# Turning attention weights by DMA as two 16-bit planes, and making low halves with an adding DMA

## The chip, the core and the metric

The kernel runs on one core of a Trainium2 chip. The metric is device time in microseconds of one execution. TensorE (PE) does matmuls, VectorE (DVE), ScalarE (ACT) and GpSimd (POOL) do elementwise work, and SyncE (SP) issues most DMAs. PEld is TensorE's weight load.

## The reference

The kernel computes one layer of a hybrid encoder on a sequence of 512 frames with 1024 channels, in float32. The core of the reference, cut to what matters here:

```python
# branch A: sparse attention, per head of 64 channels, in blocks of 128 queries
dots  = einsum('thd,sd->ths', q_idx, k_idx) * IDX_DIM ** -0.5
score = einsum('th,ths->ts', w_idx, relu(dots))            # -inf beyond the query's chunk
_, sel = top_k(score, n_sel)
logits = einsum('thd,tnhd->htn', q, k[sel]) * HEAD_DIM ** -0.5 + bias
p = softmax(logits)
yA = einsum('htn,tnhd->thd', p, v[sel])
# branch B: stick-breaking attention
z = einsum('thd,shd->hts', q, k) * HEAD_DIM ** -0.5
log_keep = where(causal, log_sigmoid(-z), 0)
later = cumsum(log_keep, reverse) - log_keep
a = where(causal, exp(log_sigmoid(z) + later), 0)
yB = einsum('hts,shd->thd', a, v)
# both branches: projection, sigmoid gates, output projection, LayerNorm; then a gated conv FFN, LayerNorm
```

Both branches have eight heads. All their queries, keys, values and gates come from one input projection. A weighing (the last product of each branch) needs the weights with keys on the partitions, so the 512 x 512 triangle of a head's weights, which is computed with queries on the partitions, has to be turned.

## The kernel before

**Products.** Each float32 operand is split into a high half (rounded to the matmul's format) and a low half (the rest). A product is three matmuls: high weight by high x (line 223), high weight by low x (224), low weight by high x (225). Weights come in pieces of 128 x 1024 through the class `Stream`: a load on SP's queue (line 71) into a ring of three `raw` tiles, ScalarE's copy to `whi` (line 101) and a subtraction `wlo = raw - whi` (line 103), in rings of three. The pieces are loaded and split three ahead of their use. For the 19 pieces named in `POOL_LO` (queries, keys and gates of the stick-breaking branch, one query, one key and four value pieces of the sparse one) GpSimd does the subtraction, for all others VectorE.

**Order.** `FILL` lists the projection pieces. Around and between the 16 heads, eight stick-breaking (`s`) ahead of eight sparse ones (`a`), the calls `fill(GAP)` pour 15 of their matmuls. From these the scheduler of the compiler makes each engine's queue by a timeline that it simulates, so small pieces can interleave. A head goes through `start_head` (logits, and for a sparse head the whole softmax), `turn_weights` and `weigh`; head i + 1 is started before head i is turned and weighed.

**Turning and weighing.** A head's weights are 128 x 1280: four query blocks j with 128 (j + 1) key columns each, at the columns `OFF[j]`. `turn_weights` does ten transposes of 128 x 128 on TensorE (line 410) into three PSUM banks (`tr_ps`), and from each bank ScalarE makes a high half `pth` (line 414) and VectorE a low half `ptl` (line 415). `weigh` takes eight matmuls (line 426): for each key block i the columns 128 i to 512 of the queries, high and low. ScalarE and VectorE then add the two column halves into `avt` and `ytmp`.

**The sparse head.** `dsa_head` loads a window of relative biases `win`, GpSimd adds the mask from the selection into `bm` (line 479), TensorE makes the logits `l_ps` (line 490), VectorE adds bias and finds the extreme (494), ScalarE takes the exponential in place (496) and VectorE normalises (502); the result is the tile `lg`.

**A turn by DMA that is already there.** Between attention and FFN the normalised rows `r` are turned as two 16-bit planes: ScalarE copies a plane (line 742, `own`), SP issues a transposing DMA (743, `got`), ScalarE or VectorE copies it back (750, `back`), and the halves `x1h` and `x1l` are made (752, 753).

**Other names.** `ks_ps` and `gb_ps` are PSUM banks of projections; `va` and `vs` are the value tiles, `ga` and `gb` the gates, `ya` and `ys` the weighed pairs of heads. `ln` is LayerNorm's parameters, `s_win` and `s_line` are a DRAM scratch for the relative bias.

Of the kernel before, what the change touches and what calls it, by code (L numbers as in the profile page):

```python
# [11 lines left out]
F32 = mybir.dt.float32  # L12
F32R = mybir.dt.float32r
# [38 lines left out]

class Stream:


    def __init__(self, tc, raw, ring, pieces, ahead_load, ahead_split, place=None, lo_on_pool=()):
# [5 lines left out]
        self.lo_on_pool = set(lo_on_pool)  # L62
# [23 lines left out]
    def _advance(self, upto):  # L86
        nc = self.nc
        n = len(self.pieces)
        self.load(min(n, upto + self.al))
        while self.ns < min(n, upto + self.asp, self.nl):  # L90
            t, w = self.loaded.pop(self.ns)
            key = self.pieces[self.ns][0]
            if key in self.place:
                hi, lo = self.place[key](key)
            else:
                hi = self.ring.tile([128, 1024], F32R, tag="whi", name=f"whi_{self.ns}")
                lo = self.ring.tile([128, 1024], F32R, tag="wlo", name=f"wlo_{self.ns}")
            after = None
            if key in self.prepare:
                w, after = self.prepare[key](t)  # L100
            nc.scalar.activation(hi[:, :w], t[:, :w], AF.Copy)  # L101
            eng = nc.gpsimd if key in self.lo_on_pool else nc.vector
            self.done[key] = eng.tensor_sub(lo[:, :w], t[:, :w], r32(hi[:, :w])).ins  # L103
# [14 lines left out]
def tile_block(ctx: ExitStack, tc: tile.TileContext, xT, xN, w_qi, w_ki, w_t, w_v, w_br, w_o, w_fi, w_fo,  # L118
# [74 lines left out]
    st = Stream(tc, rawp, ring, order, 3, 3, place, POOL_LO)  # L193


    idle = bp.tile([128, 512], mybir.dt.bfloat16, tag="beta", bufs=2, name="idle")
# [5 lines left out]

    ident = cst.tile([128, 128], F32, name="ident")
    make_identity(nc, ident)
    first = bp.tile([128, 512], F32, name="first")
# [157 lines left out]
    def idx_scores():  # L363
        kih, kil, wi = index["k"]
        for j in (1, 2, 3):
            N = 128 * (j + 1)
            for h in range(H):
                yield j
                ps = pa("dot_ps")
                r = slice(j * 128, j * 128 + 128)  # L370
                nc.tensor.matmul(ps[:, :N], qi[h][:, r], kih[:, :N], start=True, stop=False)
                nc.tensor.matmul(ps[:, :N], qi[h][:, r], kil[:, :N], start=False, stop=True)
                rl = bp.tile([128, 512], F32, tag="pt", bufs=8, name="relu")
# [23 lines left out]
            pass  # L397


    def turn_weights(a):  # L400

        groups = (((0, 0),), ((1, 0), (3, 384)), ((2, 0),))
        pth, ptl = {}, {}
        for grp in groups:
            ps = pb("tr_ps")
            width = 0
            for i, o in grp:
# [1 line left out]
                    c = OFF[j] + i * 128  # L409
                    nc.tensor.transpose(ps[:, o + (j - i) * 128:o + (j - i) * 128 + 128], a[:, c:c + 128], ident)  # L410
                width = max(width, o + 512 - 128 * i)
            th = bp.tile([128, 512], F32R, tag="pt", bufs=8, name="pth")
            tl = bp.tile([128, 512], F32R, tag="pt", bufs=8, name="ptl")
            nc.scalar.activation(th[:, :width], ps[:, :width], AF.Copy)  # L414
            lows = nc.vector.tensor_sub(tl[:, :width], ps[:, :width], r32(th[:, :width]))  # L415
            for i, o in grp:
                pth[i] = th[:, o:o + 512 - 128 * i]
                ptl[i] = tl[:, o:o + 512 - 128 * i]
        return pth, ptl, lows.ins

    def weigh(pth, ptl, vt, h, ytmp):

        ps = pb("av_ps")
        seq = [(i, t) for i in range(NB) for t in (pth, ptl)]
        for n, (i, t) in enumerate(seq):
            nc.tensor.matmul(ps[:, 128 * i:512], vt[i][:, h].rearrange("p a d -> p (a d)"), t[i],  # L426
                             start=(n == 0), stop=(n == len(seq) - 1))
# [3 lines left out]
        nc.scalar.activation(tmp[own], ps[oth], AF.Copy)  # L431
        nc.vector.tensor_add(ytmp[own], ps[own], tmp[own])

    def finish_pair(ytmp, name):
        yh = xp.tile([128, 512], F32R, tag="y", bufs=12, name=f"{name}h")
# [36 lines left out]
    def dsa_head(q, k, h):  # L472
# [11 lines left out]
        for grp in ((3,), (0, 2), (1,)):  # L484
            ps = pb("l_ps")
            o = 0
            for j in grp:
                N = 128 * (j + 1)
                for hl in range(2):
                    nc.tensor.matmul(ps[:, o:o + N], q[:, hl, j * 128:j * 128 + 128], k[:, :N],  # L490
                                     start=(hl == 0), stop=(hl == 1))
                c = slice(OFF[j], OFF[j] + N)
                b = win[:, 384:512] if j == 0 else bm[:, c]
                nc.vector.tensor_tensor_reduce(out=lg[:, c], in0=ps[:, o:o + N], in1=b, scale=1.0, scalar=3.0e38,
                                               op0=ALU.add, op1=ALU.min, accum_out=mn[:, j:j + 1])
                nc.scalar.activation(lg[:, c], lg[:, c], AF.Exp, scale=-1.0, bias=mn[:, j:j + 1],
                                     accum_out=sm[:, j:j + 1])
                o += N
        nc.vector.reciprocal(rs, sm)
        for j in range(NB):  # L500
            c = slice(OFF[j], OFF[j] + 128 * (j + 1))
            nc.vector.tensor_scalar(lg[:, c], lg[:, c], rs[:, j:j + 1], None, op0=ALU.mult)
# [83 lines left out]
    def start_head(i):  # L586
# [5 lines left out]
        return sb_head(*args) if w == "s" else (dsa_head(*args),)  # L592

    weights = start_head(0)
    sb_sticks(*weights)
    fill_until("qs1", "ks1")
    for i, (w, h) in enumerate(heads):
        following = start_head(i + 1) if i + 1 < len(heads) else (None,)
        fill(GAP)
        pth, ptl, lows = turn_weights(weights[0])  # L600
        if len(following) == 2:
            with tc.issue_after(lows):
                scan = sb_sticks(*following)
            with tc.issue_after(scan):
                select_some(ROUNDS[i])
        fill(GAP)
        if h % 2 == 0:
            ytmp = bp.tile([128, 512], F32, tag="yt", bufs=2, name=f"y{w}t{h//2}")
        fill_until(f"v{w}")
        weigh(pth, ptl, vals[w], h, ytmp)  # L610
        if h % 2 == 1:
            (ys if w == "s" else ya).append(finish_pair(ytmp, f"y{w}{h//2}"))
# [524 lines left out]
```

## Time and profile before

| | |
|---|---|
| runs, median | 762.77 us (762.73 to 762.9) |
| the profiled execution | 762.16 us |
| its span | 760.4 us |
| granted TensorE clock, mean over the span | 0.998 |
| TensorE busy | 748.6 us, 98% |
| VectorE busy | 555.4 us, 73% |
| ScalarE busy | 379.3 us, 50% |
| GpSimd busy | 153.5 us, 20% |

The stages by time: until 60 us the first loads, index queries and keys; to about 205 us the stick-breaking heads; to about 330 us the sparse heads; then projections of the branches, gates, output projection and the FFN; from 690 us the tail of the FFN and the last LayerNorm. Matmuls overlap: a row's duration is longer than the distance to the next row's start, and what one costs TensorE is read from the starts.

### The profile page before, as it was taken

How to read it: one execution, taken by the hardware profiler on the slowest of the kernel's cores; microseconds unless marked ns; L12 is line 12 of the kernel's file. 1: busy time of each engine (PE TensorE's matmuls, PEld its weight loads, DVE VectorE, ACT ScalarE, POOL GpSimd, SP SyncE). 2: the span in 40 equal slices, each digit the busy share in tenths (PEclk: the TensorE clock that was granted, in tenths of full speed). 3: DMA queues.
4: the chain of work that ended last, by engine and by line, in shares of the span. 5: the costliest groups of instructions: out<-in, count | busy, mean ns of one | idle time of the engine just before them, and what ended most of it. 6: DMA issues, size and time to landing. Idle time of an engine off the chain costs nothing.

```text
span 760.4 us, 9842 instructions
## 1 busy us (share of the span) xinstructions
PE 748.6 (98%) x3573; PEld 627.3 (82%) x3573; DVE 555.4 (73%) x905; ACT 379.3 (50%) x568; POOL 153.5 (20%) x160
## 2 busy tenths in 40 slices
PE   9999999999999999999999999999999999999995
PEld 7878888887888888888889888888888888888885
DVE  5569787799878585548765867766776768668995
ACT  5474756655574756835364633433443344346430
POOL 1002555426644210000111110111011101110012
PEclk9999999999999999999999999999999999999999
DMA  8445433232223324116942344544444444448632
GB/s 267 147 128 181 125 95 96 72 111 84 80 102 111 111 76 122 64 60 206 340 61 84 139 156 136 155 137 139 153 140 142 147 138 137 141 152 274 222 105 79
DMA packets 40448, 102.89 MB, mean 135 GB/s; under 512 B 10888, under 2 KB 11272, under 8 KB 40400
## 3 DMA queue, kind: packets, MB, share of 16 engines
q1 hardware_dynamic: 34672, 85.98, 35.4%
q0 software_dynamic: 3728, 11.04, 4.0%
q10 hardware_dynamic: 2000, 5.24, 2.8%
q8 instruction: 28, 0.46, 0.3%
q14 instruction: 20, 0.16, 0.1%
HBM read 88.59 MB, written 9.98 MB: 130 GB/s over the span
## 4 chain that ended last, share of the span: by engine, by line
PE 92%; DVE 5%; issue 1%; ACT 0%; POOL 0%; POOLq 0%; ACTq 0%; DVEq 0%
PE u_ps L774 5%; PE u_ps L776 5%; PE g_ps L774 5%; PE u_ps L775 5%; PE g_ps L776 5%; PE g_ps L775 5%; PE m L856 2%; PE m L854 2%; PE m L855 2%; PE av_ps L426 2%; PE ga_ps L224 2%; PE ga_ps L223 2%; PE ga_ps L225 2%; PE o_ps L704 2%; PE o_ps L703 2%; PE o_ps L705 2%
## 5 line engine op out<-in xcount | busy, mean ns | idle before, releaser
L101 ACT ACTIVATE whi<-raw 128x1024 fp32r<-128x1024 f32 (+1 forms) x124 | 124.1, 1001 | 169.5 <-PE g_ps L775 44.9
L103 DVE TENSOR_TENSOR wlo<-raw,whi 128x1024 fp32r<-128x1024 f32 (+1 forms) x105 | 120.0, 1144 | 41.3 <-ACT whi L101 40.5
L776 PE MATMUL u_ps<-x1h,wlo 128*128 128x512 f32 (+1 forms) x192 | 71.4, 372 | 0.0
L774 PE MATMUL u_ps<-x1h,whi 128*128 128x512 f32 (+1 forms) x192 | 71.3, 372 | 0.0
L775 PE MATMUL u_ps<-x1l,whi 128*128 128x512 f32 (+1 forms) x192 | 71.3, 371 | 0.0
L774 PE MATMUL g_ps<-x1h,whi 128*128 128x512 f32 (+1 forms) x184 | 69.9, 380 | 0.0
L775 PE MATMUL g_ps<-x1l,whi 128*128 128x512 f32 (+1 forms) x184 | 69.9, 380 | 0.0
L776 PE MATMUL g_ps<-x1h,wlo 128*128 128x512 f32 (+1 forms) x184 | 69.9, 380 | 0.0
L103 POOL TENSOR_TENSOR wlo<-raw,whi 128x1024 fp32r<-128x1024 f32 x19 | 45.8, 2412 | 34.5 <-ACT whi L101 34.4
L776 PEld LDWEIGHTS u_ps<-x1h,wlo 128*128 128x128 f32 x192 | 36.2, 188 | 6.3
L775 PEld LDWEIGHTS u_ps<-x1l,whi 128*128 128x128 f32 x192 | 36.2, 188 | 6.3
L774 PEld LDWEIGHTS u_ps<-x1h,whi 128*128 128x128 f32 x192 | 36.2, 188 | 6.2
L415 DVE TENSOR_TENSOR ptl<-tr_ps,pth 128x512 fp32r<-128x512 f32 (+1 forms) x48 | 27.9, 595 | 18.2 <-ACT pth L414 17.6
L776 PEld LDWEIGHTS g_ps<-x1h,wlo 128*128 128x128 f32 x184 | 34.6, 188 | 6.6
L775 PEld LDWEIGHTS g_ps<-x1l,whi 128*128 128x128 f32 x184 | 34.6, 188 | 6.5
L774 PEld LDWEIGHTS g_ps<-x1h,whi 128*128 128x128 f32 x184 | 34.6, 188 | 6.5
L797 DVE TENSOR_TENSOR t<-raw 128x512 f32<-128x512 f32 x11 | 7.6, 693 | 40.2 <-DMA raw<-in_w_fo_dram 40.2
L816 POOL MEMSET u<- 128x2 f32 x22 | 2.1, 98 | 143.7 <-ACT whi L101 99.9
L830 DVE TENSOR_TENSOR hF<-g_ps,c 128x512 f32<-128x512 f32 x22 | 15.1, 687 | 20.4 <-PE g_ps L776 20.4
L822 ACT ACTIVATE c<-c,cwt 128x512 f32<-128x512 f32 x22 | 16.0, 725 | 26.3 <-DVE c L821 26.1
L672 POOL TENSOR_TENSOR rstd<-rstd,mhalf 128x1 f32<-128x1 f32 x8 | 7.6, 951 | 106.0 <-DVE rstd L671 106.0
L414 ACT ACTIVATE pth<-tr_ps 128x512 fp32r<-128x512 f32 (+1 forms) x48 | 23.9, 520 | 9.8 <-PE tr_ps L410 6.8
(566 smaller groups left out, 2055.9 us busy)
## 6 DMA issues: line engine op xcount, KB each, us to landing
raw<-in_w_fi_dram SPq DMA_DIRECT2D x44, 512.0 KB, 3.3
raw<-in_w_t_dram SPq DMA_DIRECT2D x32, 512.0 KB, 3.4
raw<-in_w_fo_dram SPq DMA_DIRECT2D x26, 512.0 KB, 4.2
raw<-in_w_br_dram SPq DMA_DIRECT2D x8, 512.0 KB, 3.3
raw<-in_w_o_dram SPq DMA_DIRECT2D x8, 512.0 KB, 4.2
raw<-in_w_v_dram SPq DMA_DIRECT2D x7, 512.0 KB, 3.9
raw_b<-in_w_fo_dram SPq DMA_DIRECT2D x6, 512.0 KB, 4.2
s_t<-t POOLq DMA_DIRECT2D x11, 256.0 KB, 2.3
```

What stands on the lines that cost most here:

```text
L101: nc.scalar.activation(hi[:, :w], t[:, :w], AF.Copy)
L103: self.done[key] = eng.tensor_sub(lo[:, :w], t[:, :w], r32(hi[:, :w])).ins
L223: nc.tensor.matmul(ps[:M], wh[:, c], xh[k], start=(k == 0), stop=False)
L224: nc.tensor.matmul(ps[:M], wh[:, c], xl[k], start=False, stop=False)
L225: nc.tensor.matmul(ps[:M], wl[:, c], xh[k], start=False, stop=(k == KC - 1))
L414: nc.scalar.activation(th[:, :width], ps[:, :width], AF.Copy)
L415: lows = nc.vector.tensor_sub(tl[:, :width], ps[:, :width], r32(th[:, :width]))
L426: nc.tensor.matmul(ps[:, 128 * i:512], vt[i][:, h].rearrange("p a d -> p (a d)"), t[i], start=(n == 0), stop=(n == len(seq) - 1))
L774: nc.tensor.matmul(ps[:, c], wh[:, kc], x1h[:, k, c], start=(k == 0), stop=False)
L775: nc.tensor.matmul(ps[:, c], wh[:, kc], x1l[:, k, c], start=False, stop=False)
L776: nc.tensor.matmul(ps[:, c], wl[:, kc], x1h[:, k, c], start=False, stop=(k == KC - 1))
L822: nc.scalar.activation(c, c, AF.Gelu_apprx_tanh, bias=cwt[:, f, 3:4])
```

## The change

**A. The eight sparse heads are turned by DMAs.** The ten transposes and three evictions of a sparse head go. `send_planes`, called at the end of `dsa_head`, copies the high 16 bits of `lg` (ScalarE) and the low 16 bits (VectorE) into the memory of `bm`, and SP issues two transposing DMAs (line 441) into one tile `pl`. `join_planes` copies the planes back into float32 words (`back`), and makes one high and one low half of 128 x 1280 from them. The columns of a sparse head are laid out by `SOFF`, and the transposed blocks of a key block i lie 384 columns apart; the first key block is weighed as 384 and 128 columns, so `weigh` has ten matmuls for a sparse head. A sparse head is now weighed one head later, and its joining is ordered behind the last logits of the following head. The stick-breaking heads are turned on TensorE as before, into one pair of 1280-wide tiles instead of eight 512-wide ones; tiles that used the old ones (`kih`, `kil`, `wiT`, `relu`) take others.

**B. Nineteen low halves come from an adding DMA.** For the pieces now named `DMA_LO` ScalarE writes minus the high half into `wlo` (line 104), and GpSimd issues a DMA (line 105) that reads the weights from DRAM once more and adds them onto it.

```diff
-POOL_LO = [t for t in FILL[4:] if t[:-1] in ("qs", "ks", "gb")] + ["qa0", "ka0"]
-POOL_LO += [f"va{g}" for g in range(4)]
+DMA_LO = [t for t in FILL[4:] if t[:-1] in ("qs", "ks", "gb")] + ["qa0", "ka0"]
+DMA_LO += [f"va{g}" for g in range(4)]
 OFF = {0: 0, 2: 128, 3: 512, 1: 1024}
+SOFF = {1: 0, 0: 256, 2: 384, 3: 768}
...
             nc.scalar.activation(hi[:, :w], t[:, :w], AF.Copy)
-            eng = nc.gpsimd if key in self.lo_on_pool else nc.vector
-            self.done[key] = eng.tensor_sub(lo[:, :w], t[:, :w], r32(hi[:, :w])).ins
+            if key in self.lo_by_dma:
+                nc.scalar.activation(lo[:, :w], r32(hi[:, :w]), AF.Copy, scale=-1.0)
+                self.done[key] = nc.gpsimd.dma_start(lo[:, :w], self.pieces[self.ns][1], accum_op=ALU.add).ins
+            else:
+                self.done[key] = nc.vector.tensor_sub(lo[:, :w], t[:, :w], r32(hi[:, :w])).ins
...
+    def send_planes(lg, bm):
+        src = halves16(lg)
+        own = bm[:, 0:ATT].bitcast(U16).rearrange("p (a c) -> p a c", a=2)
+        pl = bp.tile([128, 2, ATT // 128, 128], U16, tag="pl", bufs=1, name="pl")
+        nc.scalar.activation(own[:, 1], src[:, 1], AF.Copy)
+        nc.vector.tensor_copy(own[:, 0], src[:, 0])
+        for a in (0, 1):
+            nc.sync.dma_start_transpose(pl[:, a], own[:, a])
+        return pl
+
+    def join_planes(pl):
+        back = bp.tile([128, ATT], F32, tag="back", bufs=1, name="back")
+        got = pl.rearrange("p a b c -> p a (b c)")
+        nc.scalar.activation(halves16(back)[:, 1], got[:, 1], AF.Copy)
+        nc.vector.tensor_copy(halves16(back)[:, 0], got[:, 0])
+        th, tl = turned()
+        nc.scalar.activation(th, back, AF.Copy)
+        nc.vector.tensor_sub(tl, back, r32(th))
+        h, l = (t.rearrange("p (s c) -> p s c", c=128) for t in (th, tl))
+        parts = [(i, o, h[:, c], l[:, c]) for i, o, c in
+                 ((0, slice(128, 512), slice(0, 9, 3)), (0, slice(0, 128), slice(2, 3)),
+                  (1, slice(128, 512), slice(1, 9, 3)), (2, slice(256, 512), slice(5, 9, 3)),
+                  (3, slice(384, 512), slice(9, 10)))]
+        return parts
...
+        else:
+            ends = following[2:]
+            if joined is not None:
+                added = values_of(*joined)
+                ends = ends or added
+            fill(GAP)
+            with tc.issue_after(ends[0]), tc.issue_after(ends[1]):
+                parts = join_planes(weights[0])
+            joined = parts, w, h
```

On TensorE, among the last two sparse heads before, a head's transposes stand inside the other's weighing and among gate matmuls (`ga_ps`):

```order
L426 MATMUL av_ps<-ptl,va_2210 128x384
L426 MATMUL av_ps<-pth,va_2213 128x256
L410 MATMUL tr_ps<-ident,lg 128x128 x6
L426 MATMUL av_ps<-ptl,va_2213 128x256
L426 MATMUL av_ps<-pth,va_2216 128x128
L426 MATMUL av_ps<-ptl,va_2216 128x128
L410 MATMUL tr_ps<-ident,lg 128x128 x4
L223 MATMUL ga_ps<-xh_324,whi_3011 128x512
```

In the changed kernel the weighing of such a head on TensorE reads:

```order
L466 MATMUL av_ps<-ptl,va_2223 128x384
L466 MATMUL av_ps<-pth,va_2223 128x128
L466 MATMUL av_ps<-ptl,va_2223 128x128
L466 MATMUL av_ps<-pth,va_2226 128x384
L466 MATMUL av_ps<-ptl,va_2226 128x384
L466 MATMUL av_ps<-pth,va_2229 128x256
L466 MATMUL av_ps<-ptl,va_2229 128x256
L466 MATMUL av_ps<-pth,va_2232 128x128
L466 MATMUL av_ps<-ptl,va_2232 128x128
L228 MATMUL ga_ps<-xl_186,whi_3008 128x512
```

No transposes are left there, and the first key block (`va_2223`) has a piece of 384 and one of 128 columns.

On GpSimd, at the first stick-breaking heads, the subtractions before:

```order
L103 TENSOR_TENSOR wlo_719<-raw_716,whi_718 128x1024
L385 MEMSET score_370 64x64
L103 TENSOR_TENSOR wlo_791<-raw_788,whi_790 128x1024
L103 TENSOR_TENSOR wlo_828<-raw_825,whi_827 128x1024
L468 TENSOR_TENSOR beta<-beta,keep 128x1280
L103 TENSOR_TENSOR wlo_892<-raw_889,whi_891 128x1024
```

And now, with the adding DMAs in their places:

```order
L105 DMA wlo_719<-in_w_t_dram 128x1024
L389 MEMSET score_370 64x64
L105 DMA wlo_792<-in_w_t_dram 128x1024
L105 DMA wlo_830<-in_w_t_dram 128x1024
L509 TENSOR_TENSOR beta<-beta,keep 128x1280
L105 DMA wlo_895<-in_w_t_dram 128x1024
```

GpSimd's queue keeps its order; each issue takes the place of a subtraction, and waits for ScalarE's minus-high half instead of its high half.

On SP, at the last sparse heads, the loads of branch weights (`w_br`) before:

```order
L71 DMA raw_3093<-in_w_t_dram 128x1024
L71 DMA raw_3151<-in_w_br_dram 128x1024
L71 DMA raw_3197<-in_w_br_dram 128x1024
L71 DMA raw_3253<-in_w_br_dram 128x1024
L71 DMA raw_3304<-in_w_br_dram 128x1024
```

And now:

```order
L72 DMA raw_3057<-in_w_br_dram 128x1024
L72 DMA raw_3097<-in_w_br_dram 128x1024
L441 DMA_TRANSPOSE pl<-bm 128x10x128 x2
L72 DMA raw_3143<-in_w_br_dram 128x1024
L441 DMA_TRANSPOSE pl<-bm 128x10x128 x2
L72 DMA raw_3203<-in_w_br_dram 128x1024
```

The transposes stand between the loads, and a load behind them is issued after the planes that they wait for have been copied.

More of the change, by code (lines that the diff above doesn't have):

```diff
@@ L53, with __init__ @@
 class Stream:
-    def __init__(self, tc, raw, ring, pieces, ahead_load, ahead_split, place=None, lo_on_pool=()):
+    def __init__(self, tc, raw, ring, pieces, ahead_load, ahead_split, place=None, lo_by_dma=()):
         self.tc, self.nc, self.raw, self.ring, self.pieces, self.last = tc, tc.nc, raw, ring, pieces, None
@@ L61, in __init__ @@
         self.tail = len(pieces)
-        self.lo_on_pool = set(lo_on_pool)
+        self.lo_by_dma = set(lo_by_dma)
         self.al, self.asp = ahead_load, ahead_split
@@ L192, in tile_block @@
     place = {}
-    st = Stream(tc, rawp, ring, order, 3, 3, place, POOL_LO)
+    st = Stream(tc, rawp, ring, order, 3, 3, place, DMA_LO)
     idle = bp.tile([128, 512], mybir.dt.bfloat16, tag="beta", bufs=2, name="idle")
@@ L204, in tile_block @@
     make_identity(nc, ident)
-    first = bp.tile([128, 512], F32, name="first")
+    first = bp.tile([128, 512], F32, tag="pl", bufs=1, name="first")
     nc.gpsimd.memset(first, 0.0)
@@ L397, in select_some, with turned @@
             pass
+    def turned():
+        return (bp.tile([128, ATT], F32R, tag="th", bufs=1, name="pth"),
+                bp.tile([128, ATT], F32R, tag="tl", bufs=1, name="ptl"))
     def turn_weights(a):
-        groups = (((0, 0),), ((1, 0), (3, 384)), ((2, 0),))
-        pth, ptl = {}, {}
-        for grp in groups:
+        groups = ((0, ((0, 0),)), (512, ((1, 0), (3, 384))), (1024, ((2, 0),)))
+        th, tl = turned()
+        parts = []
+        for base, grp in groups:
             ps = pb("tr_ps")
@@ L411, in turn_weights @@
                 width = max(width, o + 512 - 128 * i)
[L412 to L415, printed above, removed]
+            w = slice(base, base + width)
+            nc.scalar.activation(th[:, w], ps[:, :width], AF.Copy)
+            lows = nc.vector.tensor_sub(tl[:, w], ps[:, :width], r32(th[:, w]))
@@ L416, in turn_weights, with halves16 @@
             for i, o in grp:
[L417 to L421, printed above, removed]
+                c = slice(base + o, base + o + 512 - 128 * i)
+                parts.append((i, slice(128 * i, 512), th[:, c], tl[:, c]))
+        parts.sort(key=lambda t: t[0])
+        return parts, lows.ins
+    def halves16(t):
+        return t.bitcast(U16).rearrange("p (c two) -> p two c", two=2)
@@ L423, in weigh @@
+    def weigh(parts, vt, h, ytmp):
         ps = pb("av_ps")
-        seq = [(i, t) for i in range(NB) for t in (pth, ptl)]
-        for n, (i, t) in enumerate(seq):
-            nc.tensor.matmul(ps[:, 128 * i:512], vt[i][:, h].rearrange("p a d -> p (a d)"), t[i],
+        seq = [(i, o, t) for i, o, th, tl in parts for t in (th, tl)]
+        for n, (i, o, t) in enumerate(seq):
+            dst = ps[:, o] if len(t.shape) == 2 else ps[:, o].rearrange("p (s c) -> p s c", c=128)
+            nc.tensor.matmul(dst, vt[i][:, h].rearrange("p a d -> p (a d)"), t,
@@ L430, in weigh @@
         tmp = bp.tile([128, 512], F32, tag="av", bufs=2, name="avt")
-        nc.scalar.activation(tmp[own], ps[oth], AF.Copy)
-        nc.vector.tensor_add(ytmp[own], ps[own], tmp[own])
+        moved = nc.scalar.activation(tmp[own], ps[oth], AF.Copy)
+        added = nc.vector.tensor_add(ytmp[own], ps[own], tmp[own])
+        return moved.ins, added.ins
     def finish_pair(ytmp, name):
@@ L596, in tile_block, with values_of @@
     fill_until("qs1", "ks1")
+    def values_of(parts, w, h):
+        if h % 2 == 0:
+            pair[w] = bp.tile([128, 512], F32, tag="yt", bufs=2, name=f"y{w}t{h//2}")
+        fill_until(f"v{w}")
+        ends = weigh(parts, vals[w], h, pair[w])
+        if h % 2 == 1:
+            (ys if w == "s" else ya).append(finish_pair(pair[w], f"y{w}{h//2}"))
+        return ends
+    pair, joined = {}, None
     for i, (w, h) in enumerate(heads):
-        following = start_head(i + 1) if i + 1 < len(heads) else (None,)
+        following = start_head(i + 1) if i + 1 < len(heads) else ()
         fill(GAP)
[L600 to L612, printed above, removed]
+        if w == "s":
+            parts, lows = turn_weights(weights[0])
+            if len(following) == 2:
+                with tc.issue_after(lows):
+                    scan = sb_sticks(*following)
+                with tc.issue_after(scan):
+                    select_some(ROUNDS[i])
+            fill(GAP)
+            values_of(parts, w, h)
+        else:
[3 more added lines that the diff above has]
+                ends = ends or added
+            fill(GAP)
+            with tc.issue_after(ends[0]), tc.issue_after(ends[1]):
+                parts = join_planes(weights[0])
+            joined = parts, w, h
         fill(GAP)
         weights = following
+    fill(GAP)
+    values_of(*joined)
     fill(9999)
```

23 lines of the change are left out of this document (12 added, 11 removed).

## The prediction

> **What bounds the kernel now.** I read the page first: span, busy shares, the chain by engine.
>
> ```profile
> span 760.4 us, 9842 instructions
> PE 748.6 (98%) x3573; PEld 627.3 (82%) x3573; DVE 555.4 (73%) x905; ACT 379.3 (50%) x568; POOL 153.5 (20%) x160
> PE 92%; DVE 5%; issue 1%; ACT 0%; POOL 0%; POOLq 0%; ACTq 0%; DVEq 0%
> ```
>
> TensorE is busy for 748.6 of 760.4 us and is 92% of the chain that ended last. The view by stretches, cut where the stages change, says where the other 11.8 us lie (columns: stretch, its length, busy us and instructions of PE, PEld, DVE, ACT and POOL, granted clock, DMA share, GB/s).
>
> ```profile
> 60.00:205.00 145.00, 144.06 (x715) 121.25 (x714) 124.05 (x256) 81.04 (x145) 70.91 (x44) 1.00 0.34 103
> 205.00:330.00 125.00, 124.47 (x620) 104.74 (x619) 83.21 (x165) 80.34 (x146) 27.91 (x27) 1.00 0.30 96
> 330.00:690.00 360.00, 360.00 (x1662) 301.18 (x1661) 253.94 (x341) 158.78 (x190) 42.10 (x63) 1.00 0.46 147
> ```
>
> The change acts in the first two rows: stick-breaking heads (60 to 205 us) and sparse heads (205 to 330 us). There TensorE is idle for 0.94 and 0.53 us, at full clock. So a matmul taken out shortens the run by its own pitch, and work moved to another engine costs nothing until TensorE runs out of filler. No stall is there to be removed: the 19 low halves now on GpSimd stop nobody.
>
> **Transposes.** The group of line 410 within 205 to 330 us, and TensorE's timeline in two places (start, duration, engine, line, form, count):
>
> ```profile
> L410 PE MATMUL tr_ps<-ident,lg 128*128 128x128 f32 x80 | 12.3, 272 | 0.0
> ...
> 311.65 0.40 PE L224 MATMUL ga_ps<-xl,whi 128*128 128x512 f32 x1
> 311.88 0.60 PE L410 MATMUL tr_ps<-ident,lg 128*128 128x128 f32 x4
> 312.24 0.48 PE L225 MATMUL ga_ps<-xh,wlo 128*128 128x512 f32 x1
> 312.56 0.39 PE L223 MATMUL ga_ps<-xh,whi 128*128 128x512 f32 x1
> ...
> 313.38 0.82 PE L410 MATMUL tr_ps<-ident,lg 128*128 128x128 f32 x6
> 313.95 0.48 PE L225 MATMUL ga_ps<-xh,wlo 128*128 128x512 f32 x1
> 314.26 0.39 PE L223 MATMUL ga_ps<-xh,whi 128*128 128x512 f32 x1
> ```
>
> A transpose lasts 272 ns, but what it costs is the distance between starts. Four take 312.24 - 311.88 = 0.36 us, six take 313.95 - 313.38 = 0.57 us. The matmul behind a run is followed after 0.32 and 0.31 us where an undisturbed one takes 0.23 (311.65 to 311.88): 0.09 and 0.08 us more per run. A head's ten cost 0.36 + 0.57 + 0.17 = 1.10 us, eight heads **8.8 us**. Bounds: 80 x 0.09 = 7.2 us if nothing after a run is regained, and the 12.3 us that the group was busy. I take 8.8, since it comes from the starts themselves.
>
> The Trainium skill prices this otherwise: "TensorE: Matmul & The Clock Gate", Part 4, the PE-mode transpose, gives about 275 ns for one within a kernel; by that 80 would be worth 22 us. The trace agrees with the duration (272 ns) and not with the price (0.09 us from start to start).
>
> **The weighing.** With the new column order the first key block's 512 columns go as 384 and 128: two matmuls more per head.
>
> ```profile
> 326.67 0.39 PE L426 MATMUL av_ps<-pth,va 128*128 128x512 f32 x1
> 326.90 0.39 PE L426 MATMUL av_ps<-ptl,va 128*128 128x512 f32 x1
> 327.12 0.34 PE L426 MATMUL av_ps<-pth,va 128*128 128x384 f32 x1
> 327.30 0.40 PE L225 MATMUL ga_ps<-xh,wlo 128*128 128x512 f32 x1
> ...
> 328.17 0.22 PE L426 MATMUL av_ps<-pth,va 128*128 128x128 f32 x1
> 328.23 0.28 PE L426 MATMUL av_ps<-ptl,va 128*128 128x128 f32 x1
> 328.34 0.45 PE L224 MATMUL ga_ps<-xl,whi 128*128 128x512 f32 x1
> ```
>
> Starts give 0.23 + 0.22 = 0.45 us for the two 512s, 0.18 for a 384, 0.06 and 0.11 for the two 128s. After: 2 x 0.18 + 0.17 = 0.53 us, so 0.08 more per head, **+0.6 us** in all. The 384s and 256s also read runs of 128 columns lying 384 apart. No matmul before does that: nothing if the stride is free; if each run paid the 0.11 us of a lone 128, a 384 would cost 0.33 instead of 0.18, four per head, 8 x 4 x 0.15 = 4.8 us. I take nothing, since the run's columns alone set the 0.18.
>
> **What takes the transposes' place.** The FFN entry already does the same turn through DMAs, on 1024 columns where here they are 1280.
>
> ```profile
> L742 ACT ACTIVATE own<-r x6: 1038/1042/1060, 380.6 to 400.5; 128x1024 uint16<-128x1024 uint16 x6
> L743 SPq DMA_TRANSPOSE got<-own x6: 1233/1288/1353, 381.7 to 402.0; - x6
> DMA to landing us min/median/max: 3.1/3.2/4.9
> L750 ACT ACTIVATE back<-got x6: 1339/1359/1379, 386.6 to 405.2; 128x1024 uint16<-128x1024 uint16 x6
> L752 ACT ACTIVATE x1h<-back x3: 1060/1061/1062, 389.2 to 406.6; 128x1024 fp32r<-128x1024 f32 x3
> L753 DVE TENSOR_TENSOR x1l<-back,x1h x3: 1218/1218/1226, 390.3 to 410.3; 128x1024 fp32r<-128x1024 f32 x3
> L414 ACT ACTIVATE pth<-tr_ps x48: 360/582/621, 92.2 to 323.0; 128x512 fp32r<-128x512 f32 x32, 128x256 fp32r<-128x256 f32 x16
> L415 DVE TENSOR_TENSOR ptl<-tr_ps,pth x48: 393/682/693, 92.9 to 323.7; 128x512 fp32r<-128x512 f32 x32, 128x256 fp32r<-128x256 f32 x16
> L502 DVE TENSOR_SCALAR lg<-lg,rs x32: 276/447/2628, 204.8 to 318.6; 128x128 f32<-128x128 f32 x8, 128x256 f32<-128x256 f32 x8, 128x384 f32<-128x384 f32 x8, 128x512 f32<-128x512 f32 x8
> ```
>
> Scaled by 1.25, ScalarE does per head a plane copy of 1.30, a copy back of 1.70 and the high half of 1.33 us, less three evictions (2 x 0.58 + 0.36): 2.8 us more, 22.5 in eight heads, and some 2 for the minus-high halves that fall here: 80.3 + 24.6 = 105 of the 117 us that remain. VectorE's copies do not show in their size; at ScalarE's durations it takes 1.3 + 1.7 + 1.52 - 1.75 = 2.8 us more per head as well, 83.2 + 22 = 105. Both stay under TensorE's time, at some 90%, which costs nothing as long as no chain is late.
>
> The chain that can be late, from a head's last logits: normalising 4 x 0.45 = 1.8, plane copy 1.3, two issues on SP 2 x 1.6 = 3.2, landing 3.2 x 1.25 = 4.0, copy back 1.7, high half 1.3, low half 1.5: 14.8 us. In the changed order 89 to 163 TensorE instructions stand between a head's last logits and the first product of its weighing; at 0.22 us that is 19.6 to 36 us, and the two last heads are the tight ones with about 5 us to spare. So nothing is charged, with little cover there; one tile for the planes means that a late head also delays the next one's transposes. Weight loads queue on SP behind transposes that wait for their copies: three pieces of 24 matmuls are loaded ahead, 3 x 24 x 0.23 = 16.6 us against such a wait of about 3 us and two issues. After the last weighing 14 TensorE rows stand ahead of the branch product that needs it (31 before): 3.2 us for a copy, a sum and two halves; I take 0.2 us. The tiles that change names (one pair for a stick-breaking head's turned weights instead of eight small tiles, six instead of eight for the rectified index scores) are free again before they are filled, since a head's weighing stands ahead of the next head's transposes on TensorE: 0, covered by the 15 filler matmuls in between. The idle 0.5 to 0.9 us that VectorE and ScalarE cause before stays.
>
> **The 19 low halves.** Line 103 on GpSimd becomes one more pass on ScalarE (about 1.06 us as in line 752, 19 x 1.06 = 20 us spread over 60 to 240 us, where it is busy for 81 of 145 us) and a transfer of 512 KB that adds onto it. GpSimd's row; its tightest and a usual piece with their first use on TensorE; and landing times:
>
> ```profile
> L103 POOL TENSOR_TENSOR wlo<-raw,whi 128x1024 fp32r<-128x1024 f32 x19 | 45.8, 2412 | 34.5 <-ACT whi L101 34.4
> 69.42 2.40 POOL L103 TENSOR_TENSOR wlo<-raw,whi 128x1024 fp32r<-128x1024 f32 x1
> 77.16 0.39 PE L225 MATMUL ks_ps<-xh,wlo 128*128 128x512 f32 x1
> 114.02 2.41 POOL L103 TENSOR_TENSOR wlo<-raw,whi 128x1024 fp32r<-128x1024 f32 x1
> 129.13 0.40 PE L225 MATMUL gb_ps<-xh,wlo 128*128 128x512 f32 x1
> raw<-in_w_t_dram SPq DMA_DIRECT2D x32, 512.0 KB, 3.4
> L663 POOL DMA_DIRECT2D ln<-in_lnp_dram x4: 527/562/597, 362.3 to 410.7; - x4
> DMA to landing us min/median/max: 4.1/5.5/8.2
> s_win<-s_line POOLq DMA_DIRECT2D x1, 2048.0 KB, 15.3
> ```
>
> From GpSimd's start to the first use are 7.7 us for the tightest (a key projection), 15.1 for a usual one. The new way needs 1.1 for the pass, 0.56 for the issue and a landing. No transfer before adds; the nearest are 512 KB queued by GpSimd, 5.5 us (4.1 to 8.2), so 7.1 us, which fits everywhere: **0 us**. Ends: 3.4 us for a plain load, 15.3 for the longest. Up to 8 us of landing at most the tightest piece is late, by some 2 us; at 15.3 the 19 pieces, with slacks of 7.7 to 15 us, together fall short by about 64 us, of which some overlap: +50 us. GpSimd itself loses 46 us of work; nobody waited for it, so that gives nothing.
>
> **Sum.** Profiled execution 762.16 us (span 760.4) - 8.8 + 0.6 + 0.2 = 754.2. The median of the runs is 762.77, 0.6 above the profiled one: **754.8 us**.
>
> **Rivals.** (1) The turned weights come late: ScalarE and VectorE at 90%, three queues in series, one plane tile, 5 us to spare. Half a microsecond to 1 us of waiting in each of eight heads gives back 4 to 8 us: 758 to 763, about 760. Against it: long cover in six heads. (2) The adding transfer lands late; slower than before. It decides where landing passes about 10 us, when the tighter half of the pieces falls short by more than the 8 us gained; at 15.3 it gives 754.8 + 50 = 805. For it: the transfer reads weight and destination, and it shares VectorE's busiest stretch (124 of 145 us). The Trainium skill, "SBUF — State Buffer", on the two separate sides, has such a DMA's descriptors wait while VectorE holds the port that it shares with GpSimd, 620 ns becoming 3100; and "Collectives: The Full Stack", on the bandwidth ceiling, says an add costs two source reads. Against: GpSimd's issues at line 663 take 0.53 to 0.60 us beside VectorE's work. (3) The transposes are worth their full 272 ns: 21.8 instead of 8.8 us, 754.8 - 13 = 742; the pitch in the timeline speaks against it. (4) Strided runs cost as lone matmuls: +4.8, 759.6, inside the range.
>
> **Chances.** Forecast 64% (own range 753 to 758), late weights 17%, late adding transfer 13%, full price of transposes 3%, strided runs 3%. Leaving out the slow transfers that end above 764 and the full price, 752 to 763.5 holds 8 in 10. 0.2%, 761.2 to 764.3, is about what a measurement here can tell from no change. Slower: most of the adding transfer's 13% and a corner of late weights, 16%; same: the upper end of late weights and a mild late transfer, 8%; faster 76%.
>
> **What would show it.** Right: no line 410 rows after the stick-breaking heads; TensorE's busy time down by about 8; no wait of TensorE over 1 us between 60 and 330 us; the FFN stretch unchanged at 360 us. Wrong: waits of the weighing for ScalarE or VectorE in the last heads (rival 1), or of key, query, gate or value products for a DMA on the low half, with landings over 10 us (rival 2), or starts 0.33 us apart behind the strided 384s (rival 4).

## The result, and the profile after

The changed kernel took 770.31 us (766.55 to 770.75), the kernel before, timed beside it, 762.75: a ratio of 1.009, interval 1.0074 to 1.0105. It is 0.9% slower, where 754.8 us was forecast. The profiled execution took 770.57 us. First its page: span, busy shares, and the chain that ended last by engine.

```profile
span 768.8 us, 9804 instructions
PE 746.0 (97%) x3509; PEld 623.9 (81%) x3509; DVE 564.0 (73%) x905; ACT 417.5 (54%) x587; POOL 128.2 (17%) x160
PE 88%; DMA 4%; ACT 4%; DVE 1%; issue 1%; POOL 0%; POOLq 0%; ACTq 0%
```

TensorE's busy time fell by 2.6 us and not by 8, and DMA and ScalarE have entered the chain. The same three stretches as before:

```profile
60.00:205.00 145.00, 142.66 (x699) 119.84 (x698) 122.90 (x254) 97.49 (x162) 45.31 (x46) 0.99 0.69 163
205.00:330.00 125.00, 118.50 (x550) 99.81 (x549) 87.57 (x161) 98.03 (x142) 28.21 (x27) 0.97 0.60 143
330.00:690.00 360.00, 357.96 (x1654) 299.27 (x1653) 253.95 (x340) 159.70 (x191) 42.15 (x63) 1.00 0.44 144
```

TensorE now idles in all three, and the granted clock is 0.97 in the sparse heads where it was 1.00. The view of waits says for what it idled (total, times, longest):

```profile
PE gb_ps L229 <- DMA wlo<-in_w_t_dram: 6.5, 2, 4.3
PE va_ps L249 <- DMA wlo<-in_w_v_dram: 2.2, 1, 2.2
PE av_ps L466 <- ACT pth L451: 1.8, 1, 1.8
```

Three of the 19 adding DMAs land too late (a value piece and gates 6 and 7), and the last sparse head's high half does. What a wait leaves behind shows in TensorE's timeline around the value piece:

```profile
200.04 0.94 PE L248 MATMUL va_ps<-whi,xh 128*128 128x512 f32 x3
203.17 0.79 PE L249 MATMUL va_ps<-wlo,xh 128*128 128x512 f32 x1 [2.19 <-DMA wlo<-in_w_v_dram]
203.76 0.63 PE L250 MATMUL va_ps<-whi,xl 128*128 128x512 f32 x1
204.19 0.63 PE L249 MATMUL va_ps<-wlo,xh 128*128 128x512 f32 x1
...
206.59 0.39 PE L250 MATMUL va_ps<-whi,xl 128*128 128x512 f32 x1
206.82 0.40 PE L248 MATMUL va_ps<-whi,xh 128*128 128x512 f32 x1
```

After 2.19 us of idleness matmuls start 0.43 us apart (203.76 to 204.19) until 206.3, and then 0.23 again (206.59 to 206.82).

The account against before, by the starts of matmuls: the last matmul starts 6.9 us later (758.9 instead of 752.0). Gaps longer than 0.15 us sum to 11.9 instead of 2.5 us (+9.4), and the transposes less the extra matmuls were worth 8.2 by the prediction. 6.9 - 9.4 + 8.2 leaves 5.7 us for matmuls that start late behind those gaps. Directly read, those at half rate are late by 4.4 us; the rest is a remainder, part of it 0.16 us of refilling behind each gap. From the last matmul's end to the end of the span it is 9.6 instead of 8.1 (+1.5). 6.9 + 1.5 = 8.4 is what the span grew by.

Why the adding DMAs of the gates are late stands on GpSimd's timeline and at their issue line:

```profile
238.99 3.15 POOL L520 TENSOR_TENSOR bm<-win,score 128x256 f32<-128x256 f32 x3 [2.30 <-DMA pl<-bm]
242.08 1.32 POOL L105 DMA_DIRECT2D wlo<-in_w_t_dram  x1
248.37 0.86 POOL L105 DMA_DIRECT2D wlo<-in_w_t_dram  x1 [4.96 <-ACT wlo L104]
...
L105 POOL DMA_DIRECT2D wlo<-in_w_t_dram x15: 848/869/1320, 69.9 to 248.4; - x15
DMA to landing us min/median/max: 5.1/5.7/10.6
q0 software_dynamic: 6464, 21.00, 11.5%
```

Gate 6's DMA stands in GpSimd's queue behind mask sums that wait until the transposing DMA has read `bm`. Gate 7's waits for ScalarE's minus-high half and then needs until 259.0, some 10.6 us; two transposing DMAs were issued shortly before it (243.4 and 246.0) and three loads of SP during its flight. Which of them slowed it is not shown. An adding transfer also occupies the DMA engines for longer: the queue grew by 9.96 MB and by 11.5% - 4.0%, about 58 us of all 16 engines, 3.0 us for 512 KB. In the kernel before the same queue of GpSimd's DMAs had this row:

```profile
q0 software_dynamic: 3728, 11.04, 4.0%
```

That is 30 us for 11.04 MB, 1.4 us for 512 KB. "Collectives: The Full Stack" of the Trainium skill, in the section on the bandwidth ceiling, says of the reducing step of a ring that its add needs two source reads. The factor of two fits that without showing it: the bytes counted for the adds are those of one read, and the transfers compared are not alike.

### The profile page after: what moved, and what is told of

Read it like the earlier page. It is cut to its first block, busy times and chain, and to the rows that moved or that the text cites. A ratio compares the mean times of both kernels' runs of the same rounds, so it can differ in the third digit from the quotient of the medians.

```text
span 768.8 us, 9804 instructions
## 1 busy us (share of the span) xinstructions
PE 746.0 (97%) x3509; PEld 623.9 (81%) x3509; DVE 564.0 (73%) x905; ACT 417.5 (54%) x587; POOL 128.2 (17%) x160
## 3 DMA queue, kind: packets, MB, share of 16 engines
q0 software_dynamic: 6464, 21.00, 11.5%
## 4 chain that ended last, share of the span: by engine, by line
PE 88%; DMA 4%; ACT 4%; DVE 1%; issue 1%; POOL 0%; POOLq 0%; ACTq 0%
PE u_ps L834 5%; PE u_ps L833 5%; PE g_ps L833 5%; PE u_ps L832 5%; PE g_ps L834 5%; PE g_ps L832 5%; DMA wlo<-in_w_t_dram 2%; PE m L913 2%; PE m L912 2%; PE m L914 2%; PE av_ps L466 2%; PE o_ps L761 2%; PE o_ps L763 2%; PE o_ps L762 2%; PE gb_ps L229 2%; PE gb_ps L227 2%
## 5 line engine op out<-in xcount | busy, mean ns | idle before, releaser
L107 DVE TENSOR_TENSOR wlo<-raw,whi 128x1024 fp32r<-128x1024 f32 (+1 forms) x105 | 122.8, 1170 | 39.6 <-ACT whi L102 39.1
L520 POOL TENSOR_TENSOR bm<-win,score 128x256 f32<-128x256 f32 (+2 forms) x24 | 29.7, 1273 | 31.1 <-DMA pl<-bm 25.4
L229 PE MATMUL gb_ps<-xh,wlo 128*128 128x512 f32 x64 | 25.5, 399 | 6.5 <-DMA wlo<-in_w_t_dram 6.5
L888 DVE TENSOR_TENSOR hF<-g_ps,c 128x512 f32<-128x512 f32 x22 | 15.1, 687 | 18.4 <-PE g_ps L834 17.6
L392 DVE MAX8 m<-score 128x8 f32<-128x256 f32 (+2 forms) x48 | 26.5, 554 | 1.0
L393 DVE MATCH_REPLACE8 score<-m,score 128x256 f32<-128x256 f32 (+2 forms) x48 | 26.1, 543 | 0.1
L509 POOL TENSOR_TENSOR beta<-beta,keep 128x1280 f32<-128x1280 f32 x8 | 19.6, 2451 | 37.5 <-DVE keep L507 37.5
```

Of the source, the lines that this page charges most:

```text
L107: self.done[key] = nc.vector.tensor_sub(lo[:, :w], t[:, :w], r32(hi[:, :w])).ins
L229: nc.tensor.matmul(ps[:M], wl[:, c], xh[k], start=False, stop=(k == KC - 1))
L392: nc.vector.max(m8, sc)
L393: nc.vector.match_replace(sc, m8, sc, TAKEN)
L509: nc.gpsimd.tensor_mul(beta, beta, keep[:, 1:ATT + 1])
L520: nc.gpsimd.tensor_add(bm[:, SOFF[j]:SOFF[j] + N], win[:, 512 - N:512], score[j])
```

## The experiments

**First four: which part is it?** Each was timed beside the kernel before (762.52 us). `a_turns_only` is the changed kernel with the subtraction on GpSimd again:

```diff
-            if key in self.lo_by_dma:
-                nc.scalar.activation(lo[:, :w], r32(hi[:, :w]), AF.Copy, scale=-1.0)
-                self.done[key] = nc.gpsimd.dma_start(lo[:, :w], self.pieces[self.ns][1], accum_op=ALU.add).ins
+            eng = nc.gpsimd if key in self.lo_by_dma else nc.vector
+            self.done[key] = eng.tensor_sub(lo[:, :w], t[:, :w], r32(hi[:, :w])).ins
```

> The changed kernel, but the 19 low halves are subtracted on GpSimd as before; the sparse heads are turned by DMAs. Theory (the two parts hurt each other in the sparse heads): 753 to 756 us, no wait of TensorE for a low half, granted clock near 1.00 from 60 to 330 us. Rival A (the turn by DMA is itself late and eats its gain): 759 us or more, with waits of the weighing for ScalarE or VectorE. Rival B (the adding transfers are late by themselves): as the theory here, 753 to 757.

767.52 us, 1.0069 (1.0051 to 1.0086). The theory of that moment, that the two parts only hurt each other, fell: part A alone loses (the last runs say by what). `b_adds_only` puts the three removed lines into the kernel before:

> The kernel before, but the 19 low halves come from adding DMAs; all heads are transposed on TensorE. Theory: 762 to 765 us, since landings near 5.7 us fit into the slack of 7 to 15 us when no transposing DMA and no wait for its buffer stands beside them; one stall of 1 to 2 us at most. Rival A: 762 to 765 as well. Rival B: 767 to 773, with several waits of TensorE for low halves.

763.06 us, 1.0003 (0.9995 to 1.0012), with TensorE idle for nothing between 60 and 330 us. Nineteen adding DMAs beside transposes on TensorE are hidden. `c_adds_early` keeps twelve of them in the changed kernel:

```diff
+LATE_LO = ["va0", "va1", "va2", "va3", "gb5", "gb6", "gb7"]
+DMA_LO = [t for t in DMA_LO if t not in LATE_LO]
...
+                eng = nc.gpsimd if key in LATE_LO else nc.vector
```

> The changed kernel, but the seven last of the 19 low halves (four value pieces and gates 5, 6 and 7), which fall at or in the sparse heads, are subtracted on GpSimd; twelve stay adding DMAs in the stick-breaking heads. Theory: the three stalls of 2.2, 2.2 and 4.3 us and the clock dips behind them go: 754 to 759 us. Rival B: the twelve others stall too, 763 or more. Rival A: 764 or more.

763.51 us, 1.0011 (1.0002 to 1.002): 6.8 less than the changed kernel, but above the 754 to 759 expected. None of the twelve is waited for, so rival B fell in its reason too; a new wait of 3.0 us stands there, and the last head's is left. `d_free_bm` frees GpSimd's mask sums of the transposing DMA:

```diff
-        lg = bp.tile([128, ATT], F32, tag="beta", bufs=2, name="lg")
+        lg = bm[:, 0:ATT]
...
-        own = bm[:, 0:ATT].bitcast(U16).rearrange("p (a c) -> p a c", a=2)
+        own = bp.tile([128, 2, ATT], U16, tag="beta", bufs=2, name="own")
```

> The changed kernel, but the logits are written back into the mask tile bm and the two planes go into the tile that held the logits, so GpSimd's mask sums no longer wait until a transposing DMA has read bm. Theory: GpSimd's waits for the transposing DMA (25.4 us, 5 times) go, the adding DMA of gate 6 is issued up to 4 us earlier and its stall of 2.2 us goes; the stall of gate 7, whose transfer took 10.6 us to land beside transposes and loads, may stay: 761 to 767 us. Rival (only the slow landings matter, not GpSimd's queue): 768 to 771. Rival A: 768 to 771.

765.5 us (761.58 to 769.12), 1.0037 (1.002 to 1.0054), in the range: GpSimd's wait for `pl` is gone and gate 6's wait with it; gate 7's (1.7 us) and the value piece's (3.6 us) stay.

The 3.0 us in `c_adds_early` come along a line of queues. Rows of VectorE, GpSimd, ScalarE and TensorE there:

```profile
236.82 4.52 DVE L546 TENSOR_SCALAR lg<-lg,rs 128x128 f32<-128x128 f32 x4
234.09 3.95 POOL L523 TENSOR_TENSOR bm<-win,score 128x256 f32<-128x256 f32 x3 [2.14 <-DMA pl<-bm]
238.00 2.39 POOL L110 TENSOR_TENSOR wlo<-raw,whi 128x1024 fp32r<-128x1024 f32 x1
241.43 1.27 ACT L441 ACTIVATE bm<-lg 128x1280 uint16<-128x1280 uint16 x1 [4.77 <-POOL win L519]
253.18 2.08 PE L534 MATMUL l_ps<-ka2a,qa2a 128*128 128x512 f32 x6 [3.00 <-DVE ka2a L324]
```

Four multiplies take 4.52 us beside GpSimd's work, where the same four later take 1.27. ScalarE's plane copy waits for them (they end at 241.34; the releaser in its row is inferred), ScalarE idles for 4.77 us, and behind it in the same queue stand the evictions that the next head's logits need.

**Next four: the mask sums, and the last head.** `e_turns_free_bm` is `a_turns_only` with the edit of `d_free_bm`, `f_early_free_bm` is `c_adds_early` with it. The kernel before took 762.22 us beside these four.

> Turns by DMA alone (low halves subtracted on GpSimd as before), with the logits written back into bm and the planes in the tile of the logits, so that GpSimd's mask sums do not wait for the transposing DMA. Theory C (the mask sums, released by the transposing DMA's read, fall onto VectorE's normalising, and in-order queues pass the delay on): the waits of GpSimd for the planes go, the stall of the logits for VectorE (1.2 us) goes; the stalls of 4.2 us at 192 us and 2.0 us at the last head need not: 760 to 765 against 767.5. Theory D (the load of ScalarE and VectorE and the single pair of turned tiles make joins late, whatever GpSimd does): 766 to 769.

768.52 us, 1.0084 (1.0072 to 1.0096): outside the range of theory C and inside that of theory D. The waits of 4.2 and 2.0 us stay, and that of the logits is 1.9 us.

> The kernel with twelve early adding DMAs and seven late subtractions on GpSimd, and with bm free of the transposing DMA. Theory C: the stall of 3.0 us of the logits for VectorE at 253 us and the slow clock behind it go, 763.5 becomes 756 to 760; the last head's 1.9 us stay. Theory D: 762 to 765.

760.31 us, 0.9975 (0.9966 to 0.9984): the 3.0 us are gone, 0.3 above the range of theory C, and the first version that is faster than before. `g_last_on_pe` turns the last sparse head on TensorE (the lines that give this head the old columns are left out here):

```diff
+            if h == H - 1:
+                parts, _ = turn_weights(weights[0])
+            else:
+                with tc.issue_after(ends[0]), tc.issue_after(ends[1]):
+                    parts = join_planes(weights[0])
```

> As the run before it in this call, and the last sparse head is transposed on TensorE. Costs 1.1 us of transposes; both theories: TensorE's wait of 1.9 us for the last head's high half goes, with about 0.8 us of slower matmuls behind it, so about 1.5 us less than that run.

756.45 us, 0.9927 (0.9914 to 0.994), 3.9 less than `f_early_free_bm` where 1.5 was expected. What the last head waits for stands on ScalarE's and TensorE's timeline of `f_early_free_bm` and, last, of the changed kernel:

```profile
318.55 0.60 ACT L474 ACTIVATE avt<-av_ps 64x512 f32<-64x512 f32 x1
319.05 1.63 ACT L451 ACTIVATE back<-pl 128x1280 uint16<-128x1280 uint16 x1
321.39 1.27 ACT L454 ACTIVATE pth<-back 128x1280 fp32r<-128x1280 f32 x1 [0.70 <-DVE back L452]
322.71 0.69 PE L469 MATMUL av_ps<-pth,va 128*128 128x384 f32 x1 [2.65 <-ACT pth L454]
...
334.36 0.45 PE L466 MATMUL av_ps<-pth,va 128*128 128x384 f32 x1 [1.85 <-ACT pth L451]
```

The copy back starts behind `avt`, the end of the previous head's weighing, as `join_planes` is ordered, and 1.63 + 0.70 + 1.27 us follow before the first product can start. The wait of 2.65 us has 1.7 us of slow matmuls behind it, which the expectation had at 1.9 and 0.8.

> The kernel with twelve early adding DMAs, without GpSimd's sums of bias and selection mask (the logits get the bias window alone, so the selection is left out). Theory C: VectorE's four multiplies take 1.3 us in every head instead of up to 4.5, the stall of 3.0 us at 253 us goes: 755 to 759. Theory D: the stalls stay, 762 to 765.

`h_no_mask_sums` is `c_adds_early` without GpSimd's mask sums, so that it leaves out the selection: 763.76 us, 1.0015 (1.0004 to 1.0026). A multiply took 0.49 us at most and the 3.0 us were gone, so the chain above is right. But another wait of 2.6 us, of a gate for VectorE's value eviction, came in its place: the time did not fall, and the expectation of theory C missed. The twelve times lie in two groups, 761.5 to 762.5 us at a granted clock of 0.995 and 764.4 to 765.2 at 0.990, with one between: the same waits cost more or less with the clock behind them.

**Last five: what the adds do, and what the order does.** The first three start from `g_last_on_pe`: `i_all_adds` has 19 adding DMAs, `j_no_adds` none, and `k_all_on_pe` none and every sparse head on TensorE (`h >= 0` in place of `h == H - 1`). The kernel before took 762.83 us beside these three, so times of different groups are compared by their distance from it.

> The best kernel so far (bm free, last sparse head on TensorE, twelve early adding DMAs: 756.45 us), but with all 19 adding DMAs. If the seven late ones are a cost of their own: TensorE waits for low halves of va3, gate 6 or gate 7, 2 to 6 us with the slow clock behind them, 759 to 764. If they only hurt through GpSimd's wait for the planes, which is gone: 755 to 758.

760.59 us, 0.9967 (0.9954 to 0.9979): waits of 2.5 us for a value piece and 2.0 for a gate. The kernel is 2.2 us under the kernel before where `g_last_on_pe` is 5.8 under: the seven late adds cost 3.5 us of their own even with `bm` free.

> The same kernel without any adding DMA, all 19 low halves subtracted on GpSimd. If the adding DMAs only ever cost: 755 to 757. If GpSimd's subtractions beside VectorE's scans are what makes the stall of 4.2 us at 192 us that both kernels with turns alone had: that stall and its slow clock are there again, 762 to 765.

765.28 us, 1.0039 (1.0026 to 1.0051): the wait of 4.2 us at 192 us is there again. So the twelve early adds are worth 8.2 us in this order (2.4 above the kernel before, where `g_last_on_pe` is 5.8 under it).

> As the run before it, and all eight sparse heads are transposed on TensorE, in the changed order and with the changed tiles; nothing is turned by DMA in the heads. If the stall at 192 us comes from the order and the single pair of turned tiles, and not from the turn by DMA, it is there too: 765 to 770. If it comes from the turn by DMA: 761 to 764, as the kernel before.

772.28 us, 1.0125 (1.0112 to 1.0138), above the 765 to 770 expected. Order and tiles alone, with nothing turned or added by DMA in the heads, cost 9.5 us. Against `j_no_adds` it prices seven heads turned by DMA: 772.28 - 765.28 = 7.0 us, where the prediction's 1.10 - 0.08 us per head give 7.1. In the two profiles gaps are 0.5 us longer in `j_no_adds` and slow matmuls 0.6 us shorter, so most of it is the turn; that it agrees to 0.1 us is luck (`j_no_adds` ran from 764.47 to 767.46).

`l_single_pair` takes the one pair of tiles into the kernel before (762.59 us beside these two), with three tiles for the rectified scores, whose lines are left out here; `m_relu_tiles` takes only the changed kernel's six tiles for those scores:

```diff
+        TH = bp.tile([128, ATT], F32R, tag="th", bufs=1, name="pth")
+        TL = bp.tile([128, ATT], F32R, tag="tl", bufs=1, name="ptl")
...
-            th = bp.tile([128, 512], F32R, tag="pt", bufs=8, name="pth")
-            tl = bp.tile([128, 512], F32R, tag="pt", bufs=8, name="ptl")
+            th, tl = TH[:, base:base + width], TL[:, base:base + width]
```

> The kernel before, with the one pair of 1280-wide tiles for a head's turned weights instead of eight small ones (index keys in the same pair, three tiles for the rectified scores); all heads on TensorE in the order before, low halves on GpSimd. If the single pair makes the stall of 4.2 us at 192 us and the slow clock behind it: 767 to 773, with VectorE's four scans at 5.1 us there. If it comes from the other moved tiles or from the order: 762 to 764.

> The kernel before, with only the rectified index scores in the six tiles of the changed kernel. If the single pair is the cause: 762 to 764, as the kernel before. If the tiles of the rectified scores are: 767 to 773.

771.51 us, 1.012 (1.0104 to 1.0135), and 763.04, 1.0006 (0.9997 to 1.0015). The tiles of the scores are out, and the pair makes the wait at 190 us:

```profile
PE va_ps L244 <- DVE ka1b L318: 4.0, 1, 4.0
```

But it does not make all of the 9.5 us. By the count of matmuls, TensorE of `l_single_pair` is 3.7 us late at 87 us already. That is this run's own: with its three tiles the index scores take 21.6 us from first to last start, 18.0 before. The wait of 4.0 us and the slow matmuls behind it are the pair's, 4.8 us. `k_all_on_pe` has a second wait, of 2.9 us at 219 us for VectorE's value eviction, where the kernel before waits for 0.5 and `l_single_pair` not at all; with what follows it, it costs some 4 us. Which part of the order makes that one is not shown, and that 8.9 lies near 9.5 is chance.

VectorE's four scans and its second key eviction, and GpSimd's subtraction, in the kernel before, in `k_all_on_pe` (with its two waits) and, last, in `g_last_on_pe`, show how the order makes the wait at 190 us:

```profile
183.56 3.97 DVE L466 TENSOR_TENSOR_SCAN keep<-keep,first 128x128 f32<-128x128 f32 x4
188.85 0.69 DVE L318 TENSOR_TENSOR ka1b<-ka_ps,ka1b 64x512 fp32r<-64x512 f32 x1
182.31 2.40 POOL L103 TENSOR_TENSOR wlo<-raw,whi 128x1024 fp32r<-128x1024 f32 x1 [3.16 <-ACT whi L101]
```

```profile
184.50 5.10 DVE L509 TENSOR_TENSOR_SCAN keep<-keep,first 128x128 f32<-128x128 f32 x4
190.92 0.69 DVE L324 TENSOR_TENSOR ka1b<-ka_ps,ka1b 64x512 fp32r<-64x512 f32 x1
185.27 2.67 POOL L109 TENSOR_TENSOR wlo<-raw,whi 128x1024 fp32r<-128x1024 f32 x1 [4.64 <-ACT whi L103]
PE va_ps L250 <- DVE ka1b L324: 4.2, 1, 4.2
PE gb_ps L229 <- DVE va L259: 2.9, 1, 2.9
```

```profile
183.45 0.69 DVE L325 TENSOR_TENSOR ka1b<-ka_ps,ka1b 64x512 fp32r<-64x512 f32 x1
185.71 2.96 DVE L510 TENSOR_TENSOR_SCAN keep<-keep,first 128x128 f32<-128x128 f32 x4
181.43 2.41 POOL L110 TENSOR_TENSOR wlo<-raw,whi 128x1024 fp32r<-128x1024 f32 x1 [1.32 <-ACT whi L104]
```

The scans take 2.96 us with GpSimd's subtraction over at 183.84, 3.97 with 1.15 us of it beside them, and 5.10 with all of it: 0.8 to 0.9 us for each us of it. "SBUF — State Buffer" of the Trainium skill, in the section on the two separate sides, calls this a lock on the port that the two engines share, no slowdown in proportion; these three rows come near that. With the single pair the scheduler puts a stick-breaking head's turning later on ScalarE, the next high half comes behind it, and so the subtraction falls onto the scans.

In the first two kernels the key evictions stand behind the scans in VectorE's queue, and a value product waits for their PSUM bank: from 188.75 to 189.69 in the kernel before, from 187.54 to 191.76 in `k_all_on_pe`. Of the 3.3 us more, the length of the scans is 1.1; they also start 0.9 us later, and TensorE arrives 1.2 us earlier. In `g_last_on_pe` the key evictions stand ahead of the scans, and the wait is gone. So it is in every run with adding DMAs, `b_adds_only` and the changed kernel among them, and in none without. The early adds are thus worth their 8.2 us through the order that the scheduler makes of VectorE's queue; the subtraction beside the scans of `g_last_on_pe` is no adding DMA either.

## Why the prediction was wrong, point by point

- **The transposes, 8.8 us less 0.6: right.** 7.0 us for seven heads measured, 7.1 by the prediction, closer than the runs' spread allows one to tell. The full price of 272 ns each was not seen.
- **Strided runs: right.** In `c_adds_early` a 384 in three runs of 128 takes 0.17 us (308.31 to 308.48), as a contiguous one did; rival 4 is out.

```profile
308.31 0.33 PE L469 MATMUL av_ps<-ptl,va 128*128 128x384 f32 x1
308.48 0.28 PE L469 MATMUL av_ps<-pth,va 128*128 128x256 f32 x1
```

- **The adding DMA's price was right, its cover was wrong: the step that failed first.** The sum has 0 us for the 19 low halves, since a landing "fits everywhere". Landing was 5.7 us in the median (5.5 assumed), and the tightest piece waited for 0.15 us. But the slacks of 7.7 to 15.1 us were read from the profile before and kept for the changed order. There ScalarE's high half of gate 7 ends 6.3 us ahead of its first use (246.65 to 252.98), gate 6 queues behind mask sums, and the value piece's transfer is still in flight when the next one is issued (196.0 and 198.0 us). Waits of 2.2, 2.2 and 4.3 us followed. That is rival 2 in its place of waiting, but not in its reason: only one landing passed 10 us, and it came at three pieces of the sparse heads and not at the tight early ones.
- **GpSimd's issue** took 0.87 us in place of 0.56. "SBUF — State Buffer" of the Trainium skill, in the section on the two separate sides, gives 3100 ns for such a DMA beside VectorE; no issue here came near it (1.32 us at most).
- **The renamed tiles, priced at 0: wrong.** In the order without adding DMAs the single pair made a wait of 4 us; in the changed kernel the key evictions stand ahead of the scans, and it does not show.
- **Late weights (rival 1), charged with nothing: wrong at the last head.** The chain was counted from the last logits, 14.8 us against 19.6. The one that mattered starts at the previous head's weighing, because `join_planes` is ordered behind it: wait 1.85 us.
- **The price of a wait: missing.** The sum held no term for slower matmuls behind a wait, 4.4 us at half rate here, and none for the longer tail, 1.5 us.
- **ScalarE's and VectorE's load** came out at 98.0 and 87.6 of 125 us. VectorE's copies back took 0.90 us, below ScalarE's 1.66, so they were overpriced.

Not settled: what GpSimd does in the longer tail (last section), why gate 7's transfer took 10.6 us, and why the wait of 1.9 us for the second key eviction stays in `e_turns_free_bm` and `j_no_adds`.

The chain of causes as measured, each as the distance from the kernel before beside it: order and tiles +9.5 (`k_all_on_pe`); seven heads turned by DMA -7.0, to +2.4 (`j_no_adds`); twelve early adds -8.2, to -5.8 (`g_last_on_pe`, 756.45 us, the best); seven late adds +3.5, to -2.2 (`i_all_adds`); the last head by DMA +5.2, to +3.0 (`d_free_bm`); `bm` read by the transposing DMA +4.6, to +7.6 (the changed kernel). The last three do not simply add up: undone in the other order, the late adds are worth 6.6 us (`c_adds_early`), `bm` 2.9 (`f_early_free_bm`) and the last head 3.9.

## What to carry to other kernels

A slack read from a profile belongs to that order of instructions: where a change moves work on in-order queues, count the cover again in the new order, from whatever releases each step, a shared buffer included. When TensorE is the bound, taking work off it pays by the pitch of its starts, but behind a wait of 2 us or more 1.7 us and more of slow matmuls can follow, so the last few waits decide. Look at where in a queue the awaited result stands before blaming the speed of what is ahead of it. Keep GpSimd's elementwise work off the stretches in which VectorE's results are waited for, and put a long-latency transfer only where no queue ahead of it waits for another transfer.

## What was unexpected of the hardware

The granted clock falls by a grid of time, and not by the length of a wait alone. In the changed kernel it is 0.50 from 203.11 to 206.52 and from 257.72 to 264.55, which is 3.41 us and twice that. Stretches of 3.41 us, counted back from such a start, in the changed kernel and, the last two, in `h_no_mask_sums` (columns as in the prediction; behind the stretch and its length, TensorE's busy time):

```profile
199.69:203.11 3.42, 1.29 (x7) 0.72 (x5) 2.64 (x6) 2.03 (x4) 2.32 (x2) 1.00 1.04 268
203.11:206.52 3.41, 3.35 (x8) 2.67 (x9) 2.94 (x7) 0.87 (x3) 0.17 (x1) 0.50 1.02 247
244.07:247.48 3.41, 1.57 (x7) 0.96 (x6) 2.44 (x3) 3.36 (x5) 0.00 (x0) 1.00 1.03 171
247.48:250.89 3.41, 3.03 (x13) 2.54 (x14) 2.38 (x4) 3.34 (x5) 0.86 (x1) 1.00 1.20 248
322.59:326.00 3.41, 1.43 (x7) 0.89 (x6) 2.00 (x3) 2.73 (x3) 0.00 (x0) 1.00 0.44 154
326.00:329.41 3.41, 3.41 (x10) 2.64 (x9) 2.10 (x2) 0.39 (x1) 0.00 (x0) 0.50 0.12 18
```

TensorE idles for 2.13 us of the first stretch, and the next runs at half. It idles for 1.84 us of the third, since the wait of 2.21 us that ends at 247.86 falls into two stretches, and the next runs at full. In `h_no_mask_sums` a wait of 1.98 us lies in one stretch whole and is followed by half rate, while one of 1.99 in `a_turns_only` is split and is not. In all fifteen profiles, between 10 and 740 us, the fourteen stretches at full rate with 1.98 us or more of idleness were each followed by half rate, and none with 1.84 us or less was: the limit lies between 54% and 58% of a stretch. A stretch at half rate that is full of matmuls costs 1.7 us. "TensorE: Matmul & The Clock Gate" of the Trainium skill, in Part 1, describes half rate after an idle window of about 3.4 us that runs freely; the half rate (0.43 against 0.23 us) and the window agree, while less than a whole window of idleness brought it here.

GpSimd's elementwise work delays VectorE's scans by 0.8 to 0.9 of its own overlap (2.96, 3.97 and 5.10 us above).

Each adding DMA lengthens the end of the program by 0.08 us: from the last matmul's end to the end of the span it is 8.1 us in every run without one, 9.06 with twelve (`c_adds_early`, `f_early_free_bm`, `g_last_on_pe`) and 9.64 with nineteen (the changed kernel, `b_adds_only`, `i_all_adds`). The time lies behind GpSimd's last row of work; what it does there is not shown.
